# One transpose per up stage, additions split by bank, and three more couples by seven in a ConvGLU encoder on one Trainium2 core

## The chip, the core and the metric

The kernel runs on one core of one Trainium2 chip. A core has TensorE (PE: matmuls, with a separate row for its weight loads, PEld), VectorE (DVE), ScalarE (ACT), GpSimd (POOL), SyncE (SP, which issues transfers here) and sixteen DMA engines between the chip's memory and the core's own. The metric is the device time of one execution in microseconds (us), lower is better. The kernel before takes 2399.69 us, the median of three runs (2399.18 to 2400.01).

## What is computed

A trunk of two layers over 256 tokens and a model width of 2048, all in float32. Each layer adds a token mixer and then a gated MLP to the running sum `h`. The mixer is an mLSTM in layer 0 and an HGRN2 recurrence in layer 1. The change touches the MLP alone:

```python
def conv_glu(hn, w_up, conv_w, conv_b, w_down):
    u = hn @ w_up                                  # 2048 -> 2 * 5504
    a, v = jnp.split(u, 2, axis=-1)
    ap = jnp.pad(a, ((0, 0), (1, 1), (0, 0)))      # along the tokens
    c = conv_b
    for j in range(3):
        c = c + ap[:, j:j + s] * conv_w[j]
    return (jax.nn.gelu(c, approximate=False) * v) @ w_down

for layer in range(2):
    h = h + mixer(rmsnorm(h, norm_mix_g[layer]))
    h = h + conv_glu(rmsnorm(h, norm_ffn_g[layer]), ...)
return rmsnorm(h, final_g)
```

## The kernel before

**Float32 from two halves.** A weight tile `raw` is split into `wh` (rounded by ACT to TensorE's fast 32-bit format, line 170) and `wl` (the rest, by DVE, line 171), and the activations likewise into a high and a low half. A product is then three matmuls: high by high, high by low, low by high.

**Three parts.** The 5504 hidden columns are 43 tiles of 128, and an MLP works through them in three parts, of 16, 16 and 11 tiles. A part is an up stage and then a down stage.

**An up stage** has one chunk per tile. A chunk loads 2 MB of `w_up`, and for each of 16 blocks k of the model width issues, for its two outputs a and v, one matmul of 512 columns with `wh` (line 441: the high and the low half of the 256 tokens side by side) and one of 256 columns with `wl` (line 444). Such a couple of matmuls, 441 and 444, is called a *pair of matmuls* below: 32 in a chunk. When a chunk is done, DVE and ACT add the halves, apply the convolution, the GELU and the gate, and split the result for the down stage (`done_up`, lines 1107 to 1134).

**The transpose.** At a place that the table `RESETS` names (a chunk of the part and a k), line 428 issues one PE transpose of a constant identity into a scratch bank. Nobody reads it. It is one weight load and one matmul of 128 columns between two pairs of matmuls. The table before names two places per up stage.

**A down stage** multiplies the part's gated tiles by `w_down`, in two *pairs* of output columns (`Pair`, c = 0 for the first 1024 columns and c = 2 for the rest). `stream_pair` walks through the tiles two by two, by a plan with one letter for each couple of tiles:

- N: a couple in the plain way, eight products of 512 columns, 24 matmuls. H is a single tile, 12 matmuls.
- S: the same couple with seven products, 21 matmuls, from sums of the weights (`pair_sums`, lines 234 to 236, on DVE) and sums of the activations (`forms`, lines 459 to 466).
- P: as S, but the sums of the weights come ready from memory. They are made during the part's up stage, in halves: POOL fetches half of a couple's weights (`fetch_half`, lines 249 and 250) in one chunk, DVE and ACT make and split the sums in the next (`sum_half`, lines 257 to 260), and POOL stores them (line 262). The table `MAKE` names the chunks in which halves are fetched. In the down stage POOL loads the sums back, four transfers of 512 KB for each couple (line 282), into four buffers `pr0` to `pr3` that exist once.

A pair accumulates in four PSUM banks: `c11` and `c12` are the two banks of a tile `c1`, `c21` and `c22` of a tile `c2`. Two such tiles exist, so the next pair takes over the same ones. Three further banks m1, m6 and m7 hold products that the last S or P of the plan needs: after it, `middle` (lines 1156 to 1158 and 1182) combines them and adds them to `h` while the plan's remaining N and H run. At the pair's end `done` adds the four banks to `h` (line 1187, two additions of 1024 columns). In the second layer the last part has only the pair c = 0, and the remaining columns go by plain chunks.

**Order.** The order on each engine is fixed when the program is built: a scheduler places the instructions by its own estimate of their durations, and each engine then runs its list strictly in that order, waiting on semaphores. Weights are loaded by SP's queue into three buffers, in the order of the chunks; POOL's queue carries the fetches, stores and loads of the sums.

Of the kernel before, what the change touches and what calls it, by code (L numbers as in the profile page):

```python
# [12 lines left out]
ALU = mybir.AluOpType  # L13
# [5 lines left out]
KT = D // P  # L19
FT = 5504 // P  # L20
PARTS = ((0, 16), (16, 16), (32, 11))
RESETS = (((2, 1), (9, 1)), ((0, 3), (6, 1)), ((0, 3), (6, 1)))
A = "PSNSPSNN"
A2 = "PSNSPSNN"
B = "PSNNNH"
B2 = "PSNNNH"
DOWN_PLAN = {16: A, 11: B}
DOWN_PLAN2 = {16: A2, 11: B2}
MAKE = {16: (0, 2, 3, 5, 6, 8, 9, 11), 11: (0, 2, 3, 5)}
AH = 8  # L30
BH = 16
EPS = 1e-6
# [33 lines left out]
def trunk_kernel(ctx, tc, xT, x_d, fg_d, pp_d, cst_d, sel_d, w_gate, w_first, w_aq, w_ak, w_av, w_ao, w_aout,  # L66
                 w_bq, w_bv, w_bg, w_bout, w_up, w_down, w_last, out, mscr, sums):
    nc = tc.nc
    act, dve, pool, pe = nc.scalar, nc.vector, nc.gpsimd, nc.tensor
# [14 lines left out]
    hm = hx.rearrange("p k t -> p (k t)").rearrange("p (a c) -> p a c", a=2)  # L84
# [582 lines left out]
    def mlstm(norm, nxt, after):  # L667
# [23 lines left out]
        def gates(ps):  # L691
            with tc.tile_pool(name="gt", bufs=1) as gp:
# [18 lines left out]
                dve.tensor_tensor(lf, lf, e, ALU.add)  # L711
                B = gp.tile([H, T], F32, tag="l", name="B")
                pool.memset(B, 0.0)
                f_, b_ = slice(0, 32), slice(32, 64)
                scan = dve.tensor_tensor_scan
                scan(B[f_, 128:256], ones[f_, 128:256], lf[f_, 128:256], 0.0, ALU.mult, ALU.add)
                scan(B[f_, 126::-1], ones[f_, 0:127], lf[f_, 127:0:-1], 0.0, ALU.mult, ALU.subtract)
                scan(B[b_, 127::-1], ones[b_, 0:128], lf[b_, 127::-1], 0.0, ALU.mult, ALU.add)
                scan(B[b_, 129:256], ones[b_, 0:127], lf[b_, 128:255], 0.0, ALU.mult, ALU.subtract)
# [370 lines left out]
    def ffn(layer, norm, nxt):  # L1090
        stack = ExitStack()
        box = {}
        chunks = []
# [8 lines left out]
        def end():  # L1102
            box["prx"].__exit__(None, None, None)
            if last:
                nxt.begin(stack.enter_context(tc.tile_pool(name="fin", bufs=1)), sums_tile(box, "fg"))

        def done_up(f, i, GT, ahead):
            def go(ps):
# [23 lines left out]
                GT.half = None  # L1132
                if i in MAKE[GT.nf]:
                    j = MAKE[GT.nf].index(i)
                    if j // 2 < len(ahead):
# [25 lines left out]
        for part, (f0, nf) in enumerate(PARTS):  # L1161
            GT = Gated(nf)
            final = last and part == len(PARTS) - 1
            made = [{} for _ in range(2)]
            ahead = []
            for c in range(1 if final else 2):
                for i, kind in enumerate((DOWN_PLAN, DOWN_PLAN2)[c][nf]):
                    if kind == "P":
                        made[c][i] = numbers.pop()
                        ahead.append((made[c][i], w_down[layer, c][:, (f0 + 2 * i) * 1024:(f0 + 2 * i + 2) * 1024]))  # L1170

            for i in range(nf):
                chunks.append(Chunk("fm", w_up[layer, f0 + i], KT, norm.x, done_up(f0 + i, i, GT, ahead)))
                chunks[-1].reset = dict(RESETS[part]).get(i)
                chunks[-1].apart = bool(part) and i == 0
            for c in (0, 2):
                def middle(acc, c=c):
                    at = wpool.tile([P, 2048], F32, tag="raw", bufs=RAW, name="at").rearrange("p (t c) -> p t c", t=2)
                    combine(acc, at, 512)
                    for t in range(2):  # L1180
                        h = hm[:, t, 512 * c:512 * c + 1024]
                        dve.tensor_tensor(h, h, at[:, t], ALU.add)

                def done(acc, c=c, part=part):
                    for t in range(2):
                        h = hm[:, t, 512 * c:512 * c + 1024]
                        dve.tensor_tensor(h, h, acc["rows"][t], ALU.add)  # L1187
                    if part == len(PARTS) - 1:
                        if last or c:
                            end()  # L1190
                        nxt.add(c)
                        nxt.add(c + 1)
                if final and c == 2:
                    continue
                ch = Pair(w_down[layer, c // 2][:, f0 * 1024:(f0 + nf) * 1024], (DOWN_PLAN if c == 0 else DOWN_PLAN2)[nf], GT.get, GT.form, done, middle)
                ch.made, ch.box = made[c // 2], box
                chunks.append(ch)
            if final:
                def done(ps):
                    for t in range(2):  # L1200
                        h = hm[:, t, 1024:1536]
                        dve.tensor_tensor(h, h, ps[t], ALU.add)
                    nxt.add(2)
                for c in (2, 3):
                    chunks.append(Chunk("tm", w_last[c - 2], nf, GT.get, done))
                chunks[-1].last, chunks[-1].half = True, nxt.half
                chunks[-1].apart = chunks[-2].apart = True
# [15 lines left out]
    chunks = mlstm(n0, n1, begin0)  # L1223
    chunks += f0
    c = hgrn(n2, n3, begin1)
# [117 lines left out]
```

## Time and profile before

| What | Before |
|---|---|
| median of three runs | 2399.69 us |
| the profiled execution: its own time, its span | 2402.44 us, 2400.4 us |
| busy share of the span: PE, PEld, DVE, ACT, POOL | 99, 85, 81, 56, 13% |
| up stages of layer 0 (16, 16, 11 tiles), from | 402, 656, 916 us |
| down stages of layer 0, from and to | 574 to 656, 834 to 915, 1038 to 1097 us |
| up stages of layer 1, from | 1695, 1949, 2211 us |
| down stages of layer 1, from and to | 1867 to 1948, 2126 to 2210, 2333 to 2361 us |
| transposes of line 428 | 12, each with a duration of 0.27 us |
| clock granted to TensorE, mean | 0.998 of full speed |

The profile is of one execution. Matmuls overlap in it, so that the duration of one (0.39 us for 512 columns) is longer than the distance from its start to the next start, and a busy share of 99% says only that PE is never without an instruction. What a matmul costs is read from start to start.

### The profile page before, as it was taken

To read this page: it belongs to the slowest core of one execution; us is meant where nothing else is said; L and a number is where in the kernel's file an instruction comes from. 1 tells how busy PE (TensorE), PEld (TensorE's weight loads), DVE (VectorE), ACT (ScalarE), POOL (GpSimd) and SP (SyncE) were. 2 spreads that over 40 slices of the span, in tenths; PEclk is the share of its full clock that TensorE was granted. 3 is DMA by queue.
4 is the path that set the end of the run, shared out by engine and by line. 5 is a ranking of instruction groups with operands and counts; after the bars stand their busy time and mean duration, and the time that the engine had idled before them with its cause. 6 is when DMAs were issued, how large, how long until landed. Compare 5 with 4: busy or idle time off the path is not lost.

```text
span 2400.4 us, 37326 instructions
## 1 busy us (share of the span) xinstructions
PE 2383.1 (99%) x14212; PEld 2037.1 (85%) x14212; DVE 1940.4 (81%) x3197; ACT 1338.3 (56%) x2057; POOL 306.0 (13%) x451
## 2 busy tenths in 40 slices
PE   9999999999999999999999999999999999999998
PEld 7888888888888888888888888888888888887887
DVE  7766655888988888888888888885788888888876
ACT  6655455655556645655555555555565556654554
POOL 0100000111011110101222222220011101110100
PEclk9999999999999999999999999999999999999999
DMA  7655555888778887855455555445698768987854
GB/s 295 203 174 171 191 174 186 272 275 281 268 251 277 287 286 238 292 196 204 172 176 167 168 176 173 165 174 181 223 296 282 262 239 276 293 284 243 260 190 175
DMA packets 106019, 545.84 MB, mean 227 GB/s; under 512 B 10720, under 2 KB 11360, under 8 KB 55280
## 3 DMA queue, kind: packets, MB, share of 16 engines
q1 hardware_dynamic: 66656, 437.34, 53.2%
q0 software_dynamic: 38320, 104.94, 14.5%
q8 instruction: 111, 1.82, 0.3%
q10 hardware_dynamic: 864, 1.19, 0.1%
q14 instruction: 68, 0.56, 0.1%
HBM read 501.41 MB, written 42.01 MB: 226 GB/s over the span
## 4 chain that ended last, share of the span: by engine, by line
PE 96%; DVE 2%; DMA 2%; issue 0%; ACT 0%; SPq 0%; POOLq 0%; POOL 0%; ACTq 0%; DVEq 0%
PE mm L441 36%; PE mm L444 18%; PE c L309 11%; PE mm L422 7%; PE mm L423 7%; PE mm L424 7%; PE m L309 3%; DMA raw<-in_w_down 1%; DVE wl L171 1%; PE mm L433 1%; PE pn L790 1%; PE pd L973 1%; PE py L1022 1%; PE pz L536 0%; PE mm L435 0%
## 5 line engine op out<-in xcount | busy, mean ns | idle before, releaser
L441 PE MATMUL mm<-xt,wh 128*128 128x512 f32 x3690 | 1289.0, 395 | 0.0
L170 ACT CAST wh<-raw 128x1024 fp32r<-128x1024 f32 (+1 forms) x829 | 844.2, 1026 | 794.9 <-PE mm L441 471.7
L171 DVE TENSOR_TENSOR wl<-raw,wh 128x1024 fp32r<-128x1024 f32 (+1 forms) x829 | 989.8, 1199 | 357.8 <-ACT wh L170 351.0
L444 PE MATMUL mm<-xt,wl 128*128 128x256 f32 x3690 | 1027.1, 279 | 0.0
L441 PEld LDWEIGHTS mm<-xt,wh 128*128 128x128 f32 x3690 | 691.8, 188 | 158.4
L444 PEld LDWEIGHTS mm<-xt,wl 128*128 128x128 f32 x3690 | 693.7, 188 | 1.4
L309 PE MATMUL c<-wh,g 128*128 128x512 f32 x666 | 217.5, 390 | 0.0
L422 PE MATMUL mm<-wh,xt 128*128 128x512 f32 x480 | 188.2, 392 | 0.0
L423 PE MATMUL mm<-wl,xt 128*128 128x512 f32 x480 | 187.7, 391 | 0.0
L424 PE MATMUL mm<-wh,xt 128*128 128x512 f32 x480 | 187.3, 390 | 0.0
L309 PEld LDWEIGHTS c<-wh,g 128*128 128x128 f32 x666 | 125.2, 188 | 26.1
L309 PE MATMUL c<-wl,g 128*128 128x512 f32 x333 | 129.9, 390 | 0.0
L424 PEld LDWEIGHTS mm<-wh,xt 128*128 128x128 f32 x480 | 90.2, 188 | 18.5
L422 PEld LDWEIGHTS mm<-wh,xt 128*128 128x128 f32 x480 | 90.1, 188 | 18.5
L423 PEld LDWEIGHTS mm<-wl,xt 128*128 128x128 f32 x480 | 90.2, 188 | 17.4
L476 ACT COPY b<-mm 128x256 f32<-128x256 f32 x236 | 86.4, 366 | 20.5 <-DVE z L477 6.7
L170 ACT CAST wh<-T 128x1024 fp32r<-128x1024 f32 x54 | 55.3, 1050 | 69.7 <-PE c L309 43.3
L262 POOL DMA_DIRECT2D sums<-pr x76 | 53.0, 699 | 293.9 <-ACT pr L259 156.2
L282 POOL DMA_DIRECT2D pr<-sums x76 | 41.3, 551 | 359.5 <-PE c L309 244.5
L171 DVE TENSOR_TENSOR wl<-T,wh 128x1024 fp32r<-128x1024 f32 x54 | 64.8, 1223 | 26.0 <-ACT wh L170 25.7
L249 POOL COPY pr<-a 128x1 f32<-128x1 f32 x38 | 31.1, 819 | 424.2 <-DVE a L482 246.6
L309 PE MATMUL c<-wh,F 128*128 128x512 f32 x178 | 70.2, 394 | 3.8 <-DVE hx L1187 3.8
(274 smaller groups left out, 3022.7 us busy)
## 6 DMA issues: line engine op xcount, KB each, us to landing
raw<-in_w_up SPq DMA_DIRECT2D x172, 1024.0 KB, 5.6
raw<-in_w_down SPq DMA_DIRECT2D x60, 1024.0 KB, 6.1
raw<-in_w_bq SPq DMA_DIRECT2D x48, 1024.0 KB, 4.9
sums<-pr POOLq DMA_DIRECT2D x76, 512.0 KB, 8.1
pr<-sums POOLq DMA_DIRECT2D x76, 512.0 KB, 7.5
pr<-in_w_down POOLq DMA_DIRECT2D x38, 512.0 KB, 6.7
raw<-in_w_ao SPq DMA_DIRECT2D x16, 1024.0 KB, 4.9
raw<-in_w_aout SPq DMA_DIRECT2D x16, 1024.0 KB, 4.8
```

Of the source, the lines that this page charges most:

```text
L170: act.copy(h, r)
L171: dve.tensor_tensor(l, r, h.bitcast(F32), ALU.subtract)
L249: pool.tensor_copy(b[:, 0, 0:1], after)
L262: pool.dma_start(sums[n, j].rearrange("p (i o b) -> p i o b", i=2, o=2)[:, :, o], v.rearrange("p (i b) -> p i b", i=2))
L282: pool.dma_start(z[j], sums[n, j][:, 1024 * i:1024 * i + 1024])
L309: pe.matmul(o, a, b, start=name not in begun, stop=sp and i == 2)
L422: pe.matmul(ps[t], xh, wh[:, c], start=st, stop=False)
L423: pe.matmul(ps[t], xh, wl[:, c], start=False, stop=False)
L424: pe.matmul(ps[t], xl, wh[:, c], start=False, stop=sp)
L441: pe.matmul(ps[f], wh[:, c:c + P], x, start=st, stop=False)
L444: pe.matmul(ps[f][:, 0:T], wl[:, c:c + P], x[:, 0:T], start=False, stop=sp)
L476: act.copy(b, ps[:, T:2 * T])
```

## The change

```diff
-RESETS = (((2, 1), (9, 1)), ((0, 3), (6, 1)), ((0, 3), (6, 1)))
+RESETS = ((2, 1), (0, 3), (0, 3))
-B = "PSNNNH"
-B2 = "PSNNNH"
+B = "PSNPNH"
+B2 = "PSNPNH"
-MAKE = {16: (0, 2, 3, 5, 6, 8, 9, 11), 11: (0, 2, 3, 5)}
+MAKE = {16: (0, 2, 3, 5, 6, 8, 9, 11), 11: (0, 1, 2, 3, 4, 5, 6, 7)}
@@ the up stage's chunks
-                chunks[-1].reset = dict(RESETS[part]).get(i)
+                chunks[-1].reset = RESETS[part][1] if i == RESETS[part][0] else None
@@ the end of a pair
                 def done(acc, c=c, part=part):
-                    for t in range(2):
-                        h = hm[:, t, 512 * c:512 * c + 1024]
-                        dve.tensor_tensor(h, h, acc["rows"][t], ALU.add)
+                    for name, t, o, n in (("c12", 0, 512, 512), ("c11", 0, 0, 512), ("rows", 1, 0, 1024)):
+                        h = hm[:, t, 512 * c + o:512 * c + o + n]
+                        dve.tensor_tensor(h, h, acc["rows"][1] if n == 1024 else acc[name], ALU.add)
```

The change does three things. Each up stage has one transpose instead of two: the first of the two places stays and the second goes. The addition of `c1`'s two banks to `h` becomes two additions of 512 columns, `c12` first; that of `c2` stays one of 1024. In the parts of 11 tiles the fourth couple is done by seven products instead of eight, with sums from memory: two couples in layer 0 (one in each pair), one in layer 1. Their weights are summed in the up stage: the chunks 0 to 7 of layer 0's last part each fetch a half (before: 0, 2, 3 and 5), and chunks 0 to 3 in layer 1 (before: 0 and 2).

How this stands in the engines' lists is shown at four places. First PE at the start of layer 0's second up stage. `c` is the last bank of the down stage ahead, `mm` the up stage's PSUM tile, `turn` the transpose. Before:

```order
L309 MATMUL c_5788<-wh,g_5459 128x512
L441 MATMUL mm<-xt_3112,wh 128x512 x2
L428 MATMUL turn<-cst 128x128 x2
L444 MATMUL mm<-xt_3112,wl 128x256 x2
L441 MATMUL mm<-xt_3115,wh 128x512
```

And now:

```order
L309 MATMUL c_5787<-wh,g_5457 128x512
L441 MATMUL mm<-xt_3112,wh 128x512 x2
L428 MATMUL turn<-cst 128x128
L444 MATMUL mm<-xt_3112,wl 128x256 x2
L441 MATMUL mm<-xt_3115,wh 128x512
```

In the second and third up stage of either layer the two transposes stood next to each other, although the table names two chunks for them: nothing held the second back. One of the two is left, in the same place. In the first up stage of either layer, where they stood apart, the one in chunk 2 is left as it was and the one in chunk 9 is gone.

Second, PE at the start of the second pair in layer 0's first down stage, with the semaphores that an instruction waits for. `c_5787` (before) and `c_5786` (now) are the PSUM tile `c1`, taken over from the pair ahead; `m` are the further banks. Before:

```order
L309 MATMUL m_5789<-wh,g_3979 128x512 [waits Activation_49]
L309 MATMUL c_5787<-wh,F 128x512 [waits DVE_49]
L309 MATMUL c_5787<-wl,F 128x512
L309 MATMUL c_5787<-wh,g_3854 128x512
L309 MATMUL c_5788<-pr_5757,F 128x512 [waits DVE_49]
```

And now:

```order
L309 MATMUL m_5788<-wh,g_3979 128x512 [waits Activation_49]
L309 MATMUL c_5786<-wh,F 128x512 [waits DVE_49,PE_49]
L309 MATMUL c_5786<-wl,F 128x512
L309 MATMUL c_5786<-wh,g_3854 128x512
L309 MATMUL c_5787<-pr_5755,F 128x512 [waits DVE_49]
```

The products with F go into c12, the one with g_3854 into c11. There is a wait for DVE ahead of c12 and one ahead of c2, before and now, and none of its own ahead of c11.

Third, DVE at the end of the first pair of that stage: `T` is a tile of weight sums for the next pair, `hx` is `h`. Before:

```order
L1182 TENSOR_TENSOR hx<-hx,at 128x1024
L171 TENSOR_TENSOR wl<-raw,wh 128x512 [waits Activation_49]
L234 TENSOR_TENSOR T_5801<-raw 128x1024 [waits DMAHW0_49]
L1187 TENSOR_TENSOR hx<-hx,c_5462 128x1024 [waits DVE_49,PE_49]
L1187 TENSOR_TENSOR hx<-hx,c_5463 128x1024 [waits DVE_49,PE_49]
```

And now:

```order
L1182 TENSOR_TENSOR hx<-hx,at 128x1024
L171 TENSOR_TENSOR wl<-raw,wh 128x512 [waits Activation_49]
L234 TENSOR_TENSOR T_5800<-raw 128x1024 [waits DMAHW0_49]
L1187 TENSOR_TENSOR hx<-hx,c_5460 128x512 [waits DVE_49,PE_49]
L1187 TENSOR_TENSOR hx<-hx,c_5460 128x512
L1187 TENSOR_TENSOR hx<-hx,c_5461 128x1024 [waits DVE_49,PE_49]
```

The three additions stand behind the same instructions as the two did.

Fourth, POOL in the last up stage of layer 0: copies that order a fetch behind a chunk (line 249), fetches (250), stores (262). Before:

```order
L249 COPY pr0_8918<-a_8899 128x1
L250 DMA pr0_8918<-in_w_down 128x1024
L249 COPY pr0_9043<-a_9006 128x1
L250 DMA pr0_9043<-in_w_down 128x1024
L262 DMA sums<-pr2_9033 256x1x512
L262 DMA sums<-pr3_9034 256x1x512
L262 DMA sums<-pr2_9151 256x1x512
L262 DMA sums<-pr3_9152 256x1x512
```

And now:

```order
L249 COPY pr0_8814<-a_8777 128x1
L250 DMA pr0_8814<-in_w_down 128x1024
L262 DMA sums<-pr2_8804 256x1x512
L262 DMA sums<-pr3_8805 256x1x512
L249 COPY pr0_8932<-a_8902 128x1
L250 DMA pr0_8932<-in_w_down 128x1024
L262 DMA sums<-pr2_8922 256x1x512
L262 DMA sums<-pr3_8923 256x1x512
```

A fetch and two stores now follow each other in every chunk from 1 to 7, without a chunk in between that has none.

## The prediction

> **What bounds the kernel now.** I read the busy shares first, then the chain that ended last, then PE's waits.
>
> ```profile
> PE 2383.1 (99%) x14212; PEld 2037.1 (85%) x14212; DVE 1940.4 (81%) x3197; ACT 1338.3 (56%) x2057; POOL 306.0 (13%) x451
> PE 96%; DVE 2%; DMA 2%; issue 0%; ACT 0%; SPq 0%; POOLq 0%; POOL 0%; ACTq 0%; DVEq 0%
> ```
>
> PE has work for 99% of the span and is 96% of the chain. So a matmul less is time less, an edit on another engine counts only where PE then waits, and PE's waits are few:
>
> ```profile
> PE c L309 <- DVE hx L1187: 3.8, 4, 1.1
> PE m L309 <- ACT wh L170: 1.2, 1, 1.2
> ```
>
> Columns: us in total, times, longest. The first row is the wait at which the split additions aim: four times, 3.8 us in all. With PE so full, the distance between two matmul starts matters as much as their number, and that distance is not constant:
>
> ```profile
> 418.00:495.00 77.00, 77.00 (x223) 1.00 0.86 272
> 496.00:573.00 77.00, 77.00 (x219) 1.00 0.87 282
> 1711.00:1788.00 77.00, 77.00 (x223) 1.00 0.85 269
> 1789.00:1866.00 77.00, 77.00 (x219) 1.00 0.86 282
> 663.00:740.00 77.00, 77.00 (x223) 1.00 0.81 260
> 925.00:1002.00 77.00, 77.00 (x223) 1.00 0.80 258
> ```
>
> These windows count line 441 on PE: one per pair of matmuls. Same work, full clock (the 1.00), no idle, yet 223 or 219 pairs in 77 us, 345.3 (77.00/223) or 351.6 ns (77.00/219) each: a fast and a slow rhythm, 6.3 ns a pair apart. Slow are only the second halves of the two first up stages. The switch is at 495.63 and 1788.2, where the second transpose stands; the first transposes, at 417.87 and 1710.4, leave the rhythm fast.
>
> **The change part by part.** *Six transposes fewer.* Timeline of PE: start, duration, instruction.
>
> ```profile
> 417.51 0.40 PE L441 MATMUL mm<-xt,wh 128*128 128x512 f32 x1
> 417.87 0.27 PE L428 MATMUL turn<-cst 128*128 128x128 f32 x1
> 418.32 0.40 PE L441 MATMUL mm<-xt,wh 128*128 128x512 f32 x1
> 655.99 0.62 PE L441 MATMUL mm<-xt,wh 128*128 128x512 f32 x2
> 656.45 0.38 PE L428 MATMUL turn<-cst 128*128 128x128 f32 x2
> 656.90 0.39 PE L441 MATMUL mm<-xt,wh 128*128 128x512 f32 x1
> ```
>
> From 417.51 to 418.32 lie two pairs and one transpose: 0.81 us, less 0.69 for the pairs, 0.12. From 655.99 to 656.90 lie two pairs and two transposes: 0.91, so 0.11 each. Two times 0.12 and four times 0.11 is **0.7 us** off. (The Trainium skill, "TensorE: Matmul & The Clock Gate", section "Part 4: PE-mode transpose", gives some 275 ns for one inside a kernel. The duration here agrees, 0.27, but the starts are 0.11 to 0.12 apart; by the page's figure six would be an estimated 1.65 us.)
>
> *The rhythm after them.* In layer 0's first up stage the switch to slow came with the removed transpose. Without it 222 pairs stay fast: 222 x 6.3 ns = **1.4 us** off. In layer 1 it is less plain. The two switches have one thing in common beside the place: both transposes were even ones in the program's count (the 2nd and the 8th), and the first transposes, which switched nothing, odd (the 1st and 7th). A transpose is one weight load between matmuls that otherwise come in even numbers (354 in a down stage, 252 in a shorter one, 64 in a chunk), so each turns the parity of all that follows. Now there is one per stage, and the one in layer 1's first up stage is the 4th: even. If parity decides, it switches to slow, at chunk 2 rather than 9: 14 chunks less one pair, about 446 pairs slow where 222 were: 224 x 6.3 ns = **1.4 us** on. If place decides, these 222 become fast too. I take parity, as both switches bear it out; it is only two events.
>
> The second and third up stages begin fast with two transposes side by side (the windows from 663 and 925). One alone has not been seen there. I take it as fast, price 0, and give the other case below.
>
> *Nine matmuls fewer.* Three couples go from 24 to 21.
>
> ```profile
> 574.20:655.80 81.60, 80.63 (x354) 1.00 0.77 261
> 2336.00:2360.00 24.00, 24.00 (x108) 1.00 0.67 235
> ```
>
> Line 309's matmuls come 24.00/108 = 0.222 us apart where nothing waits, and 80.63/354 = 0.228 over a whole stage. Nine of 0.225 is **2.0 us** off.
>
> *The split additions.* The end of a pair, on DVE and PE:
>
> ```profile
> 605.72 0.68 DVE L1157 TENSOR_TENSOR at<-at,m 128x512 f32<-128x512 f32 x1
> 606.31 1.22 DVE L171 TENSOR_TENSOR wl<-raw,wh 128x1024 fp32r<-128x1024 f32 x1
> 616.45 2.35 DVE L1187 TENSOR_TENSOR hx<-hx,c 128x1024 f32<-128x1024 f32 x2
> 618.71 0.68 DVE L235 TENSOR_TENSOR T<-raw,T 128x512 f32<-128x512 f32 x1
> 617.72 0.50 PE L309 MATMUL c<-wh,F 128*128 128x512 f32 x1 [0.97 <-DVE hx L1187]
> 619.44 0.84 PE L309 MATMUL c<-pr,F 128*128 128x512 f32 x3
> ```
>
> Two additions of 1024 take from 616.45 to 618.71, 1.13 each; PE's first matmul into c12 starts at 617.72, as the first ends. An addition of 512 from PSUM takes 0.59 to the next start (605.72 to 606.31), two take 1.2. Were c12 free after its own 0.6, PE could start 0.55 earlier. But in the order of now, only c12's matmul waits for DVE; that into c11, three places later, has no wait of its own, though its bank must have been read. One wait then has to cover both banks, so it is for the second addition, and the split buys nothing: it costs 1.2 less 1.13, 0.07 us, at each of four waits, **0.3 us** on. Queued behind the waiting matmul is all of PE; c2's addition ends 0.07 later as well, at 618.8, and c2's matmul at 619.44 has that covered. (The Trainium skill, "Perfetto Trace Analysis", section "Optimizing Scalar/DVE Operations", puts the access overhead of a DVE instruction at some 125 ns on PSUM. That speaks against splitting: by it an estimated 0.5 us for the four. The trace's 0.07 is less.)
>
> *The added sums of weights.* The load falls on layer 0's last up stage, whose chunks take 11.1 us:
>
> ```profile
> 948.80:959.90 11.10, 11.10 (x66) 9.70 (x65) 9.01 (x17) 6.39 (x10) 0.74 (x2) 1.00 1.05 335
> 959.90:971.00 11.10, 11.10 (x66) 9.70 (x65) 10.11 (x18) 6.92 (x10) 3.01 (x4) 1.00 0.58 191
> 971.00:982.10 11.10, 11.10 (x66) 9.70 (x65) 10.19 (x21) 6.39 (x10) 0.06 (x1) 1.00 1.01 325
> 1004.30:1015.40 11.10, 11.10 (x66) 9.70 (x65) 8.36 (x15) 6.25 (x10) 1.14 (x3) 1.00 1.05 359
> L171 DVE TENSOR_TENSOR wl<-raw,wh 128x1024 fp32r<-128x1024 f32 x39 | 47.7, 1224 | 18.7 <-ACT wh L170 18.1
> L260 DVE TENSOR_TENSOR pr<-pr,pr 128x1024 fp32r<-128x1024 f32 x4 | 4.9, 1218 | 0.0
> L234 DVE TENSOR_TENSOR pr<-pr 128x512 f32<-128x512 f32 x4 | 2.8, 690 | 0.3
> L235 DVE TENSOR_TENSOR pr<-pr,pr 128x256 f32<-128x256 f32 x4 | 1.7, 417 | 0.0
> L236 DVE TENSOR_TENSOR pr<-pr,pr 128x256 f32<-128x256 f32 x4 | 1.7, 419 | 0.0
> ```
>
> The window rows give PE, PEld, DVE, ACT and POOL busy, the clock, and DMA's share and GB/s. The second and third chunk hold a half's sums on DVE, the other two none: 10.1 to 10.2 us busy of 11.1 against 8.4 to 9.0. From the groups, a half is (4.9 + 2.8 + 1.7 + 1.7)/4 = 2.8 us, four more are 11 of the 18.7 us that DVE idles ahead of line 171 in this stretch. It fits, with 0.9 us free in each of eight chunks. The memory: a chunk's 2.1 MB of weights, a fetch of 0.52 and two stores of 0.52 make 3.7 MB in 11.1 us, 331 GB/s for seven chunks running; 325 to 359 were moved in single chunks, with a share of 1.01 to 1.05. So it fits barely, covered by three buffers loaded ahead. The sums' loads are the third risk: they are issued when a buffer comes free, and
>
> ```profile
> pr<-sums POOLq DMA_DIRECT2D x4, 512.0 KB, 9.2
> ```
>
> (issues in 594 to 600, median to landing) 9.2 us is 41 matmuls of 0.225, about the distance from release to need where the second P now follows an N and an S. Lower bound 0 (all covered), upper bound one landing uncovered by half in one pair plus a late chunk, some 3 us. I take **0.5 us** on, near the lower end, since DVE has its 0.9 us free in each chunk.
>
> *Sum.* -0.7 - 1.4 + 1.4 - 2.0 + 0.3 + 0.5 = -1.9 us. The profiled execution's own time is 2402.44, 2.75 over the median, and one stretch holds nearly all of that:
>
> ```profile
> 2126.40:2210.50 84.10, 82.19 (x353) 0.98 0.74 254
> 2172.00:2175.00 3.00, 3.00 (x9) 2.35 (x8) 3.00 (x5) 1.04 (x1) 0.02 (x1) 0.50 0.53 224
> ```
>
> This down stage took 84.1 us against 81.6 for its twin above, with PE idle for 1.9 and then a granted clock of 0.50 for three us, after a late load. The timed runs lack it. 2402.44 - 1.9 = 2400.5 for an execution with that event; without its 2.75, **2397.8 us**.
>
> **Rivals.** *Place, not parity:* layer 1's first up stage is fast throughout. For it: both switches stood in chunk 9, at k = 1, and no transpose in chunk 2 switched. Against it: the matmuls around are alike in all four places. Instead of 1.4 on it is 1.4 off: 2395.0 us.
>
> *A lone transpose leaves the second and third up stages slow* (the other side). There are 512 and 352 pairs in them, all fast now behind a doubled transpose, which leaves the parity as it was. At 6.3 ns these are 3.2 and 2.2 us. One layer so is 5.4 on, 2403.2 us; both 2408.6 us. It decides against the change from about 300 slow pairs more (1.9 us/6.3 ns), less than one such stage. For it: a transpose did switch to slow twice. Against it: it did not twice, and in these stages it stands at the very start, behind another rhythm.
>
> *Layer 0's last part runs short:* DVE at over 92% or 331 GB/s for seven chunks do not hold, and PE waits where weights come late. At the upper bound of 3 us instead of 0.5: 2400.3 us, no gain.
>
> *The split does work:* c12's matmul starts 0.55 earlier, though c2's additions, now 0.07 later, soon hold PE again; worth 0.2 to 0.4 at each wait, instead of 0.07 on: 2397.8 - 0.3 - 1.2 = 2396.3 us. Against it stands the missing wait ahead of c11.
>
> **How the numbers follow.** The forecast has 0.42, place 0.22, the lone transpose 0.20 (one layer 0.15, both 0.05), the short part 0.10, the working split 0.06. About 0.2%, 4.8 us, is what a measurement of this kernel can tell from no change: 2394.9 to 2404.5. The likeliest case alone has 2396.5 to 2400.3, by the bounds of its 0.5 us and half a us elsewhere. The range reaches down past "place", with its neighbours, to 2393.5, and up past the lone transpose in one layer to 2404.5; outside lie both layers and the tails. Faster: half of "place" and some tails where two gains meet, 0.20. Slower: both layers, a third of one layer, 0.11. The rest, 0.69, is no change that can be told.
>
> **What would show it.** Line 441 counted in 77 us windows: 223 after 496 right for layer 0's first stage; 219 soon after 1711 for parity, 223 for place; 219 after 663 or 925 for the lone transpose. PE's wait for line 1187: four times about 1.0 to 1.1, or less if the split works. In layer 0's last up stage no wait of PE, or one for line 171's `wl` or a load. Layer 0's last down stage shorter by 1.4 us (six matmuls), layer 1's by 0.7 (three). Wrong would be the forecast if the down stages' matmuls took a rhythm of their own, or if the rhythm of the HGRN2 stage moved with the parity, which I left at nothing.

## The result and the profile after

The changed kernel takes **2418.89 us**, the median of six runs (2414.24 to 2422.77); the kernel before, run beside it, 2400.12 us. The ratio is 1.0076, with a 95% interval of 1.0061 to 1.0090: the change costs about 18 us. Forecast were 2397.8 us and a range up to 2404.5. The page of the profiled execution, 2418.7 us:

```profile
span 2416.9 us, 37462 instructions
PE 2392.0 (99%) x14197; PEld 2037.8 (84%) x14197; DVE 1957.8 (81%) x3252; ACT 1344.2 (56%) x2067; POOL 325.5 (13%) x487
PE 92%; DVE 4%; DMA 3%; issue 1%; ACT 1%; SPq 0%; POOLq 0%; POOL 0%; ACTq 0%; DVEq 0%
```

The lines are the span, the busy time of each engine, and the chain that ended last. PE has fifteen matmuls fewer (14212 before) and is busy 9 us longer, and 4 points of the chain (96 to 92) have gone to others, 3 of them to DVE and DMA. Both point to the distance between matmuls and to PE's waits.

The span from stage to stage, worked out from the start of each stage's first matmul in the two traces (us):

| Stage | Before | After | Difference |
|---|---|---|---|
| start to the first down stage | 574.19 | 572.71 | -1.48 |
| layer 0, first down stage | 81.80 | 82.29 | +0.49 |
| layer 0, second up stage | 177.72 | 181.00 | +3.28 |
| layer 0, second down stage | 81.84 | 82.08 | +0.24 |
| layer 0, third up stage | 122.26 | 124.26 | +2.00 |
| layer 0, third down stage | 59.10 | 67.27 | +8.17 |
| mixer of layer 1 and its first up stage | 769.85 | 769.21 | -0.64 |
| layer 1, first down stage | 81.90 | 81.76 | -0.14 |
| layer 1, second up stage | 177.72 | 181.00 | +3.28 |
| layer 1, second down stage | 84.36 | 82.08 | -2.28 |
| layer 1, third up stage | 122.26 | 124.36 | +2.10 |
| layer 1, third down stage | 28.57 | 28.58 | +0.01 |
| the rest | 38.82 | 40.27 | +1.45 |

They sum to the 16.5 us between the two spans. The -2.28 is the late load that only the profiled execution of before had. Two groups carry the rest: the second and third up stages of both layers, **10.7 us**, and the last down stage of layer 0, **8.2 us** with six matmuls fewer. The row of layer 1's mixer holds two things: its first up stage is 1.60 us shorter (179.93 before, 178.33 after), and the mixer is 0.96 longer. The mixer differs by about that much between kernels that leave it as it is (589.6 to 590.5 us), so the 0.96 is not put down to the change. At the end came 1.5 us for which the forecast had no term.

The rhythm first. Windows of line 441 on PE, after:

```profile
496.00:573.00 77.00, 76.76 (x222) 1.00 0.88 288
1789.00:1866.00 77.00, 77.00 (x224) 1.00 0.90 289
663.00:740.00 77.00, 77.00 (x219) 1.00 0.81 256
925.00:1002.00 77.00, 77.00 (x219) 1.00 0.87 280
1970.00:2047.00 77.00, 77.00 (x219) 1.00 0.80 257
2234.00:2311.00 77.00, 77.00 (x219) 1.00 0.89 290
```

The first up stages (the upper two) are fast to their ends in both layers, where 219 stood before. The second and third, 223 before, are slow. A window also counts the matmul that runs into it from before, so 77 us over the count is a little too short a distance: from start to start a pair takes 346.7 ns in the fast rhythm and 353.3 in the slow, 6.6 apart and not 6.3.

Then PE's longest waits in the whole program, of after. Below them stands the last down stage of layer 0 by line 309 (the window, PE's busy time and count, the clock, DMA's share, GB/s), first of before, then of after:

```profile
PE c L309 <- DVE hx L1187: 6.0, 5, 1.6
PE m L309 <- DMA pr<-sums: 3.4, 3, 2.2
PE m L309 <- DVE wl L171: 1.5, 1, 1.5
```

```profile
1037.82:1096.91 59.09, 58.43 (x252) 1.00 0.59 213
```

```profile
1042.34:1109.61 67.27, 61.01 (x246) 0.97 0.82 286
```

The loads of the sums (`pr<-sums`) are a wait that did not exist. The timeline of PE shows a wait for DVE's `wl` four us into the stage and the loads' from six us on, and the window of PE behind them a granted clock of 0.58:

```profile
1046.89 0.50 PE L309 MATMUL m<-wl,g 128*128 128x512 f32 x1 [1.51 <-DVE wl L171]
1050.48 1.22 PE L309 MATMUL m<-pr,F 128*128 128x512 f32 x2 [2.15 <-DMA pr<-sums]
1054.49 0.50 PE L309 MATMUL m<-pr,F 128*128 128x512 f32 x1 [0.66 <-DMA pr<-sums]
```

```profile
1050.00:1053.00 3.00, 2.52 (x6) 0.58 1.04 386
```

With six matmuls fewer (1.35 us at 0.225) the stage lost 9.5 us. The start distances that hold its waits make up 7.0 of them beyond the usual 0.227 each, six matmuls at half clock 1.2, and many small differences the rest.

POOL's timeline says why the loads are late. These are the first and the fourth of the four loads for the plan's first couple, of before and of after:

```profile
1000.97 0.54 POOL L282 DMA_DIRECT2D pr<-sums  x1 [12.06 <-DVE pr L236]
1015.65 0.53 POOL L282 DMA_DIRECT2D pr<-sums  x1 [3.43 <-DMA sums<-pr]
```

```profile
1036.57 0.55 POOL L282 DMA_DIRECT2D pr<-sums  x1 [6.99 <-DVE pr L236]
1048.66 0.53 POOL L282 DMA_DIRECT2D pr<-sums  x1 [0.85 <-DMA sums<-pr]
```

Before, they were issued 37 to 22 us ahead of the stage (1037.8); now 6 us ahead to 6 us behind its start (1042.3). What they wait for stands in the brackets: the last half's sums on DVE (line 236), which free pr0, and the last half's store, which frees pr3. The first couple's sums had been in memory for long; it is the buffers that were not free.

### The profile page after: what moved, and what is told of

The parts are those of the page before. It is cut to its first block, busy times and chain, and to the rows that moved or that the text cites. A ratio compares the mean times of both kernels' runs of the same rounds, so it can differ in the third digit from the quotient of the medians.

```text
span 2416.9 us, 37462 instructions
## 1 busy us (share of the span) xinstructions
PE 2392.0 (99%) x14197; PEld 2037.8 (84%) x14197; DVE 1957.8 (81%) x3252; ACT 1344.2 (56%) x2067; POOL 325.5 (13%) x487
## 3 DMA queue, kind: packets, MB, share of 16 engines
q0 software_dynamic: 44176, 120.67, 16.5%
## 4 chain that ended last, share of the span: by engine, by line
PE 92%; DVE 4%; DMA 3%; issue 1%; ACT 1%; SPq 0%; POOLq 0%; POOL 0%; ACTq 0%; DVEq 0%
PE mm L441 35%; PE mm L444 18%; PE c L309 9%; PE mm L422 7%; PE mm L423 7%; PE mm L424 7%; PE m L309 3%; DVE wl L171 2%; DMA raw<-in_w_down 1%; PE mm L433 1%; PE pn L790 1%; PE pd L973 1%; PE py L1022 1%; ACT wh L170 1%; DVE hx L1182 0%
## 5 line engine op out<-in xcount | busy, mean ns | idle before, releaser
L309 PE MATMUL c<-wh,g 128*128 128x512 f32 x612 | 203.0, 390 | 0.0
L309 PEld LDWEIGHTS c<-wh,g 128*128 128x128 f32 x612 | 115.0, 188 | 24.6 <-ACT v L1155 0.5
L309 PE MATMUL c<-wl,g 128*128 128x512 f32 x306 | 119.5, 391 | 0.0
L282 POOL DMA_DIRECT2D pr<-sums x88 | 48.0, 553 | 413.1 <-PE c L309 286.8
L262 POOL DMA_DIRECT2D sums<-pr x88 | 61.1, 696 | 252.8 <-ACT pr L259 141.9
L309 PE MATMUL c<-wh,F 128*128 128x512 f32 x196 | 76.7, 392 | 6.0 <-DVE hx L1187 6.0
```

The lines of the kernel that those rows point to most:

```text
L262: pool.dma_start(sums[n, j].rearrange("p (i o b) -> p i o b", i=2, o=2)[:, :, o], v.rearrange("p (i b) -> p i b", i=2))
L282: pool.dma_start(z[j], sums[n, j][:, 1024 * i:1024 * i + 1024])
L309: pe.matmul(o, a, b, start=name not in begun, stop=sp and i == 2)
```

## The experiments

The theory drawn from these two profiles had two parts: a lone transpose leaves the second and third up stages slow (10.7 us), and the first couple's sums in layer 0's last down stage come late because the last of eight halves is late (8 to 9 us). Times below are medians, each against that of the kernel before from the same chip.

### Each part taken back

`e1` puts the second transposes back:

```diff
-RESETS = ((2, 1), (0, 3), (0, 3))
+RESETS = (((2, 1), (9, 1)), ((0, 3), (6, 1)), ((0, 3), (6, 1)))
```

> The changed kernel with the two transposes per up stage put back; the couples and the split additions stay changed. Theory (two separate losses: the slow rhythm of the second and third up stages behind a lone transpose, 3.3 + 2.0 + 3.3 + 2.1 us, and late sums for the first couple of layer 0's last down stage, 8 to 9 us): the rhythm of all up stages is that of the kernel before, the last down stage of layer 0 still takes about 67 us instead of 59, and the time is about 8 us over before, near 2408 us. Rival (the couples alone disturb everything behind them, the transposes hardly matter): the time stays near 2418 us.

Measured: 2412.15 us against 2400.79, ratio 1.0041 (1.0028 to 1.0054). The second and third up stages are back at 177.72 and 122.26 us to the hundredth; layer 0's last down stage takes 67.80. The rival, 2418, is out. Over the theory's 2408 it lies by two things left out of that figure: 1.4 us more at the program's end, as in the changed kernel, and in the profiled execution a further stretch at half clock behind a pair's end in layer 1 (that down stage took 84.0 us). Layer 0's last down stage is not made up as in `after`: PE waits 3.8 us for the loads and 0.7 for `wl`, and 10.2 us of the stage, not 3.4, ran at half clock.

`e2` puts the old couples back:

```diff
-B = "PSNPNH"
-B2 = "PSNPNH"
-MAKE = {16: (0, 2, 3, 5, 6, 8, 9, 11), 11: (0, 1, 2, 3, 4, 5, 6, 7)}
+B = "PSNNNH"
+B2 = "PSNNNH"
+MAKE = {16: (0, 2, 3, 5, 6, 8, 9, 11), 11: (0, 2, 3, 5)}
```

> The changed kernel with the old couples (plans and chunks of the sums as before); one transpose per stage and the split stay. Theory: the last down stage of layer 0 is back at 59 us, the second and third up stages of both layers stay slow (181 and 124 us instead of 177.7 and 122.3): 10.6 us on, some 3.0 off for the first up stages and 0.7 for the transposes, about 7 us over before, near 2407 us. Rival (the rhythm hangs on the changed down stages, not on the transposes): fast up stages, near 2397 us.

Measured: 2409.80 us, ratio 1.0033 (1.0022 to 1.0044). Up stages 181.00 and 124.36 us, the last down stage of layer 0 60.94. That stage takes 59.10 to 60.94 us in the seven profiles with the old couples and their old chunks, so a us of difference in it says nothing. Windows of line 441:

```profile
663.00:740.00 77.00, 77.00 (x219) 1.00 0.79 255
925.00:1002.00 77.00, 77.00 (x219) 1.00 0.79 255
```

So the two losses are separate, and each goes with its own part: transposes with the rhythm, couples with the last down stage.

`e3` is the kernel before with the split additions alone.

```diff
-                    for t in range(2):
-                        h = hm[:, t, 512 * c:512 * c + 1024]
-                        dve.tensor_tensor(h, h, acc["rows"][t], ALU.add)
+                    for name, t, o, n in (("c12", 0, 512, 512), ("c11", 0, 0, 512), ("rows", 1, 0, 1024)):
+                        h = hm[:, t, 512 * c + o:512 * c + o + n]
+                        dve.tensor_tensor(h, h, acc["rows"][1] if n == 1024 else acc[name], ALU.add)
```

> The kernel before with the split additions alone. Theory (the matmul into c12 waits for the second addition): PE's waits at the four pair ends grow by about 0.07 us each, to 1.1 us, up to 0.5 us each if the two additions also start later; 2400.4 us, at most 2402. Rival (the split frees c12 early): the four waits shrink to 0.5 us, 2398.5 us.

Measured: 2400.95 against 2400.79, ratio 0.9999 (0.9990 to 1.0008): no change that can be told. The trace can tell it. DVE's additions and PE's first matmul into c12:

```profile
616.69 2.41 DVE L1187 TENSOR_TENSOR hx<-hx,c 128x512 f32<-128x512 f32 x3
618.12 0.47 PE L309 MATMUL c<-wh,F 128*128 128x512 f32 x1 [1.16 <-DVE hx L1187]
```

From the first addition's start to the matmul are 1.43 us; before it was 617.72 - 616.45 = 1.27. With the split it is 1.42 to 1.43 in `after`, `e1` and `e2` too, at the same place; without it, 1.27 in `e4`. The matmul waits for the second addition, as the order said, and the price is 0.15 us a wait.

### The transposes alone

`e4` is the kernel before without the second transpose of the first up stages:

```diff
-RESETS = (((2, 1), (9, 1)), ((0, 3), (6, 1)), ((0, 3), (6, 1)))
+RESETS = (((2, 1),), ((0, 3), (6, 1)), ((0, 3), (6, 1)))
```

> The kernel before with one transpose in the first up stage of either layer and two in the second and third. Theory (what counts is only what stands in the stage itself): the first up stages are fast throughout, the second and third stay fast behind two transposes: 2 x 1.5 us off, near 2397 us. Rival (an odd number of transposes since the mixer shifts the rhythm that the later stages start from, and two side by side leave it as it is): the second and third up stages become slow, by up to 10 us: near 2407 us.

Measured: 2397.81 us, ratio 0.9985 (0.9976 to 0.9994). The first up stages are fast to their ends, the others stay at 177.82 and 122.26 us. This is the gain that the change contained.

`f4` has none at all, `g2` three in the second and third up stages (the third lands at the head of the second chunk):

```diff
-RESETS = (((2, 1), (9, 1)), ((0, 3), (6, 1)), ((0, 3), (6, 1)))
+RESETS = ((), (), ())
```

```diff
-RESETS = (((2, 1),), ((0, 3), (6, 1)), ((0, 3), (6, 1)))
+RESETS = (((2, 1),), ((0, 3), (6, 1), (7, 1)), ((0, 3), (6, 1), (7, 1)))
```

> The kernel before without any transpose. Theory (a lone transpose shifts the rhythm, two side by side leave it as none would): all up stages fast, 2 x 1.4 us for the first ones and 1.3 us for twelve transposes off, 2396 us. Rival (the stages start in a rhythm that two transposes mend): the second and third up stages slow, 5.4 us a layer, 2407 us.

> The kernel of e4 with three transposes in the second and third up stages: two side by side at the start, one at the head of the second chunk. Theory (a lone transpose shifts the rhythm one step, fast to slow, wherever it stands behind a fast one): both stages slow from the second chunk on, 2407 to 2408 us. Rival (two or more at the start put the rhythm right for the stage): both fast, 2398 us.

Measured: `f4` 2408.59 us, ratio 1.0028 (1.0017 to 1.0040); `g2` 2405.03 in its one run. Line 441 in `f4`, second and third up stage of layer 0, then in `g2` the same of both layers:

```profile
663.00:740.00 77.00, 77.00 (x219) 1.00 0.81 259
925.00:1002.00 77.00, 77.00 (x219) 1.00 0.80 255
```

```profile
663.00:740.00 77.00, 77.00 (x219) 1.00 0.81 259
925.00:1002.00 77.00, 77.00 (x224) 1.00 0.81 260
1970.00:2047.00 77.00, 77.00 (x219) 1.00 0.81 259
2234.00:2311.00 77.00, 77.00 (x223) 1.00 0.78 252
```

Without any transpose these stages are slow as well, in both layers, while the first up stages are fast to their ends: the theory that two side by side are as good as none has fallen, and its rival stands, that they start in a rhythm which two mend. With three, the second stage is slow and the third fast, in both layers, so neither "each shifts by one" nor "two or more are enough" holds. What is shown is a table: 0, 1, 2, 3 transposes give slow, slow, fast, slow in the second up stage, and slow, slow, fast, fast in the third. With three the place differs too, since the third stands a chunk later. By what state of PE it goes is left open.

### The couples

Three kernels on the base of `e4` ask what makes the sums late.

`f1` takes the fourth couple in the first pair alone, with six halves:

```diff
-B = "PSNNNH"
+B = "PSNPNH"
-MAKE = {16: (0, 2, 3, 5, 6, 8, 9, 11), 11: (0, 2, 3, 5)}
+MAKE = {16: (0, 2, 3, 5, 6, 8, 9, 11), 11: (0, 1, 2, 3, 4, 5)}
```

> The kernel of e4 (one transpose in the first up stage, two in the others) with the fourth couple by seven in the first pair alone: one couple in layer 0, one in layer 1; six halves in a row, in chunks 0 to 5. Theory (the sums of the first couple come late because the four buffers are busy until the last half is stored): with the last half two chunks earlier no wait for loads in layer 0's last down stage, 58.4 to 60 us; each layer 0.7 off; POOL's drain at the program's end 7.7 us instead of 5.0, if it goes by the loads of the last stage (8 instead of 4), 1.4 to 1.9 on at the end; 2398.3 us. Rival (halves in every chunk overload DVE and the memory): that stage over 64 us, 2403 us.

`f2` is `f1` with the last stage's second four loads on SP's queue:

```diff
-                        pool.dma_start(z[j], sums[n, j][:, 1024 * i:1024 * i + 1024])
+                        q = nc.sync if ch.by_sp and c else pool
+                        q.dma_start(z[j].bitcast(F32), sums[n, j][:, 1024 * i:1024 * i + 1024].bitcast(F32))
```

> As f1, with the second couple's four loads of the program's last down stage issued by SP instead of POOL. Theory (the drain at the end goes by POOL's transfers of the last stage): drain back at 5.0 us, 2396.5 us. Rival (it goes by all of POOL's transfers in the program, 15 more than in e4 less these 4): drain near 6.0 us, 2398 us.

`f3` leaves the couples as they were and only makes their sums later:

```diff
-MAKE = {16: (0, 2, 3, 5, 6, 8, 9, 11), 11: (0, 2, 3, 5)}
+MAKE = {16: (0, 2, 3, 5, 6, 8, 9, 11), 11: (4, 5, 6, 7)}
```

> The kernel of e4 with the old couples and the old number of halves, but fetched in chunks 4, 5, 6 and 7 of the parts of 11 tiles instead of 0, 2, 3 and 5. Theory (late sums): layer 0's last down stage takes 65 to 68 us instead of 59 to 61, with PE waiting for the sums' loads, 2404 to 2406 us. Rival (eight halves instead of four are what DVE and the memory can't carry): that stage stays at 59 to 61 us, 2398 us.

Measured: `f1` 2397.99 (ratio 0.9986, 0.9976 to 0.9995), `f2` 2398.16 (0.9983, 0.9974 to 0.9993), `f3` 2402.66 (1.0000, 0.9990 to 1.0010). Layer 0's last down stage, `f1` and then `f3`, and the first and fourth load of the first couple in `f3`:

```profile
1036.43:1096.97 60.54, 58.66 (x249) 1.00 0.71 245
```

```profile
1036.76:1102.02 65.26, 61.00 (x252) 0.97 0.67 230
```

```profile
1024.20 0.55 POOL L282 DMA_DIRECT2D pr<-sums  x1 [6.93 <-DVE pr L236]
1038.55 0.53 POOL L282 DMA_DIRECT2D pr<-sums  x1 [1.64 <-DMA sums<-pr]
```

Six halves in a row, made early, cost that stage no wait for a load longer than 0.2 us; its 60.54 us lie above the 58.4 to 60 expected, and with three matmuls fewer than `e4` (60.66) it is no shorter. Four made late, no more work than before, cost it 4.6 us over `e4`. Of these, 1.6 are PE's waits for the loads; a wait of 1.6 for `wl` in the second pair (0.6 in `e4`) and 3.4 us at half clock behind it make up most of the rest, and whether late sums cause these is not shown. This execution is also the longest of `f3`'s eight, 3.7 us over their median. The medians on the same chip, 4.7 us apart, agree with the stage. So the time of the last half counts, with no half more than before; whether eight halves are too much besides, `f3` can't say. In `f2` the drain at the end was not 5.0 but 6.4 us; more on that below.

Two tries to get eight halves through went wrong, each in its own way. `g1` lets the halves use another buffer, so that two of the four that the loads go to are free early:

```diff
-        b = spare(0, box).bitcast(F32).rearrange("p (a b) -> p a b", a=4)
+        b = spare(4, box).bitcast(F32).rearrange("p (a b) -> p a b", a=4)
-        t, th, tl = (spare(i, box) for i in (1, 2, 3))
-        t = t.bitcast(F32)
+        th, tl = (spare(i, box) for i in (2, 3))
+        t = tl.bitcast(F32)
```

> The kernel of e4 with the fourth couple by seven in both pairs of the parts of 11 tiles (eight halves in chunks 0 to 7, as in the changed kernel), but the halves use one further buffer and two of the four that the loads go to, so that the first couple's first two loads need not wait for the last half; the other two still do. Theory (late sums): layer 0's last down stage takes 61 to 64 us instead of 67, 2400 us with the longer drain at the end. Rival (eight halves overload DVE and the memory, whatever the buffers): 67 us, 2404 us.

Measured: 2471.20 us, ratio 1.0283 (1.0264 to 1.0301). Waits of DVE and of PE:

```profile
DVE pr L257 <- DMA sums<-pr: 101.4, 26, 8.7
PE mm L444 <- DVE wl L171: 21.2, 10, 4.4
```

The sum and its low half now share one buffer, so the next half's sum cannot begin until the store has landed, and DVE, which works strictly in order, stands there with the weights behind it. This is a flaw of the experiment and says nothing on the question; it shows what one wait at the head of DVE's list costs.

`g3` exchanges the first two couples, so that the sums are needed 21 matmuls later:

```diff
-B = "PSNNNH"
-B2 = "PSNNNH"
-MAKE = {16: (0, 2, 3, 5, 6, 8, 9, 11), 11: (0, 2, 3, 5)}
+B = "SPNPNH"
+B2 = "SPNPNH"
+MAKE = {16: (0, 2, 3, 5, 6, 8, 9, 11), 11: (0, 1, 2, 3, 4, 5, 6, 7)}
```

> The kernel of e4 with the couples of the changed kernel, eight halves, and the first two couples of each plan of the parts of 11 tiles exchanged (S P N P N H): the couple whose sums are loaded is needed 21 matmuls, 4.8 us, later. Theory (late sums): layer 0's last down stage 62 to 64 us instead of 67, about 2401 us. Rival (eight halves overload DVE, and an S at the start, whose sums DVE makes there, adds to it): 67 us or more, over 2404 us.

Measured: 2413.28 us, ratio 1.0046 (1.0031 to 1.0061); the stage 70.65 us, and the up stage ahead 126.68 instead of 122.26. My theory's 62 to 64 missed, and the rival's figures came; but the plan's new S at the start is part of that rival, so the run doesn't say which of the two it was. DVE in that up stage, of `g3`, and then of `after`:

```profile
1017.80 0.69 DVE L234 TENSOR_TENSOR pr<-pr 128x512 f32<-128x512 f32 x1 [5.10 <-DMA pr<-in_w_down]
```

```profile
1021.11 0.69 DVE L234 TENSOR_TENSOR pr<-pr 128x512 f32<-128x512 f32 x1 [4.51 <-DMA pr<-in_w_down]
```

DVE waits 4 to 5 us at the head of a half's sums for a fetch that has not landed. It does so in `after`, `e1`, `g3` and a little in `f3`, and not in `before` or `f1`. A link was missing in the theory: the next fetch goes into the same pr0 and is issued only when DVE has read the last one. In `after` the eight fetches are issued from 932.1 to 1025.8, 13.4 us apart on the mean (10.7 to 17.0), where a chunk takes 11.3. On the mean each half falls 2 us further behind, until DVE, whose list has the sums at a fixed place, stands in front of one.

`h1` gives pr0 a second copy, with eight halves and the plan of the change:

```diff
-        return box["pr"].tile([P, 1024], F32R, tag=f"pr{i}", bufs=1, name=f"pr{i}")
+        return box["pr"].tile([P, 1024], F32R, tag=f"pr{i}", bufs=1 if i else 2, name=f"pr{i}")
```

> The kernel of e4 with the couples of the changed kernel (eight halves) and a second copy of the buffer pr0, into which halves are fetched. Theory (the halves form a chain, fetch, landing, sums, next fetch, through the one buffer, about 13.4 us a half against a chunk of 11.1, so that eight fall 15 us behind, the loads of the sums come late, and DVE stands behind fetches that have not landed): fetches about 11 us apart, no wait of DVE for a fetch, the last half 10 us earlier or more; layer 0's last down stage 59 to 62 us instead of 67 to 68; 2398 to 2400 us. Rival (DVE's load of eight halves is the cause): 66 us or more, over 2404 us.

Measured: 2404.97 us (2398.97 to 2408.06), ratio 1.0013 (1.0004 to 1.0023), over the theory's 2400 and at the rival's 2404. The profiled execution is the fastest of the ten, 6 us under their median, and where the others spent these 6 us is not shown. Its first and last fetch, and what PE still waits for:

```profile
926.20 0.53 POOL L250 DMA_DIRECT2D pr<-in_w_down  x1 [0.30 <-DVE v L477]
1007.75 0.55 POOL L250 DMA_DIRECT2D pr<-in_w_down  x1 [0.30 <-POOL pr L249]
```

```profile
PE m L309 <- DMA pr<-sums: 4.5, 3, 2.4
```

Fetches are 11.65 us apart (seven steps in 81.55), DVE's wait for one is down to 1.4 us, and PE has no wait for DVE in that stage beyond the pair's end. The stage takes 64.66 us: 3 better than `e1`'s 67.80, still 4 over `e4`. But PE waits 4.5 us for the loads, not less than in `e1` (3.8); what is gone against `e1` is the wait for `wl` and the stretch at half clock. The loads are issued up to 1037.5, three us into the stage, and while the last fetch is issued 27 us ahead of the stage, against 17 in `after`, the last half's sums end only 9 us ahead of it, against 6 (7 in `e1`). That half was fetched at 1007.75, and DVE begins on it at 1021.12 without a wait for it: here the place in DVE's list sets the time, not the buffer. So the chain through pr0 explains DVE's stand in front of a fetch and two or three us of the lateness. Most of the rest goes with the last half's place in chunk 7, as in `f3`; that the load of eight halves has a part in it is not ruled out.

`i1` is `f1`, six halves, with the second copy of pr0; `i2` is `e4`, four halves and the old couples, with it. The edit is that of `h1`.

> The kernel of f1 (one transpose in the first up stages, two in the others; the fourth couple by seven in the first pair alone, six halves) with the second copy of pr0 from h1. Theory (what remained in h1, waits of 4.5 us for the sums' loads, comes from the last of eight halves being stored only at the stage's start; with six there is time): no wait for loads, layer 0's last down stage 58 to 60 us; the four pairs' ends keep the shorter waits of h1 (0.6 to 0.8 us less each); 2394.5 to 2396.5 us. Rival (a couple more in layer 0 costs in any case what it saves): 2397.5 us or more.

> The kernel of e4 (old couples, four halves) with the second copy of pr0. Theory (the shorter waits at the pairs' ends in h1 come from the second buffer, which lets loads and DVE's work fall earlier): the four down stages of 16 tiles 80.3 to 81.3 us, 2395 to 2396 us. Rival (they come from the order that the new couples bring): 81.6 us each, 2397.8 us.

Measured: `i1` **2395.07 us** (2392.41 to 2398.27) against 2400.51, ratio 0.9978 (0.9970 to 0.9987); `i2` 2395.63, ratio 0.9982 (0.9972 to 0.9991). In `i1`, the first and the last load of that stage's first couple:

```profile
989.90 0.54 POOL L282 DMA_DIRECT2D pr<-sums  x1 [4.83 <-DVE pr L236]
1019.23 0.53 POOL L282 DMA_DIRECT2D pr<-sums  x1 [2.03 <-DMA sums<-pr]
```

They are 44 to 15 us ahead of the stage (1034.0), which takes 59.66 us; PE waits for no load in it. `i1` is faster than both kernels, by 5.4 us than the one before. That a sixth half or the second buffer is worth anything over `e4` is not shown: the intervals of `e4`, `i1` and `i2` overlap. With six halves the second buffer doesn't bring the last one forward either: POOL's load behind its sums is issued 92.1 us after the up stage's start in `i1` and 91.7 in `f1`. What it does at the pairs' ends stays unclear: the four down stages of 16 tiles take 80.3 to 81.9 us in `i1` and 80.8 to 81.9 in `i2`, not the 80.3 to 81.3 that I had expected.

## Why the prediction was wrong

**What bounds the kernel** was read rightly: PE, and the rhythm as much as the count. Two of the rivals came true at once, which no case of the forecast had added up: the lone transpose in both layers (priced at 10.8 us, measured 10.7) and the short part (priced at 3 us in all, measured 9.5 with its six matmuls).

**Transposes.** 0.12 us for a lone one stands: the two pairs around the one at 417.98 take as long as before. Right in size, and nothing beside what follows.

**The rhythm of the first up stages.** Layer 0's 1.4 us came: the stage is 1.60 us shorter, 222 pairs of 6.6 ns and one transpose. Layer 1's came too, where 1.4 us on had been forecast. Parity of the program's count fell at once: the 4th transpose, an even one, switched nothing, and layer 1's first up stage is fast (224 in the window after 1789). The rival "place" had that right. Two events had been too few to prefer a rule.

**The second and third up stages.** This is the step that failed: "One alone has not been seen there. I take it as fast, price 0". It rested on reading a pair of transposes as neutral, from the parity that had been guessed for other stages. `f4` shows that they are not neutral but needed: with none the stages are slow as with one. In `after` they lost 3.28 and 2.00 us in layer 0, 3.28 and 2.10 in layer 1, where the forecast had nothing. What sets the rhythm stays open. The profile of before could not show it, since it had no stage of that kind with another number; the honest price was the rival's 5.4 us a layer with a chance near one half.

**Nine matmuls.** Their 2.0 us are not visible as such. Layer 1's last down stage is as long as before although 3 of 126 went, since two matmuls of the plain chunks (line 422) now stand inside it and some others came 231 to 338 ns apart instead of 227. From that stage's first matmul to PE's last are 57.82 us against 58.27: 0.45 of the 0.7.

**The split additions.** The mechanism was right, read from the order: one wait covers both banks. Its size was 0.15 us instead of 0.07. The sum of the durations gives the forecast's 0.07: the second short addition ends 1.28 us after the first one's start (0.60 to its own start, 0.68 long), the long one ended after 1.21. The other 0.08 lies between an addition's end and the matmul, 0.06 us before and 0.14 now, which the sum had taken as equal; why it grew is not shown.

**The added sums.** The other step that failed: "I take 0.5 us on, near the lower end, since DVE has its 0.9 us free in each chunk". The working asked whether DVE and the memory could carry eight halves on the mean, and the up stage itself bears it: it takes 122.26 us in `e1` and `h1`, as before. What was not worked out was when the last half ends, since only then the buffers of the loads are free. The term was 0.5 us, its upper bound 3; the stage lost 9.5. The risk in the loads was sought at the second couple of sums; it was the first, whose loads stand behind the last half for want of buffers. From `before`'s four halves in chunks 0, 2, 3 and 5 this could have been seen: there, too, the first load waited for line 236 of the last half, at 1000.97, 37 us ahead of need. In `after` it is issued 6 us ahead. Of the 31 us lost some 23 are the two chunks by which the last half is fetched later (chunk 7 instead of 5, 11.3 us each); the rest is drift, to which the one buffer belongs (13.4 us a half against a chunk of 11.3). `f3`, late without more halves, has the waits for loads; `f1`, with six early ones, has not. How much the load of eight halves adds by itself stays open.

**The end of the program** had no term at all: 1.9 us for POOL's drain, told below.

## What to carry to other kernels

When a kernel makes something ahead of time through shared buffers, price the latest item, not only the load: find when the last item is made and when it lets go of what the first consumer needs, by the place of its work in each engine's order and by its way from buffer to buffer, and compare with the slack that the first consumer had. An instruction without effect on data that a tuned kernel carries may set a rhythm; a count of them is tried stage by stage, and a rule from two events is no ground for a price of nothing. And where one wait covers two banks, splitting the work ahead of it only made it longer here.

## What the runs showed of the hardware

POOL's last DRAIN grew with the number of transfers that POOL issued in the whole program, in all runs but one. Instructions of the program's last line, of before and of after (durations in ns: least, median, longest):

```profile
L1325 POOLq DRAIN  x3: 46/102/5014, 2393.8 to 2400.1; - x3
```

```profile
L1325 POOLq DRAIN  x3: 46/102/7709, 2408.4 to 2416.6; - x3
```

There were 76 + 76 + 38 = 190 transfers of sums and their weights before and 220 after (and 20 others in either): 2.70 us for 30, 0.09 each. In `f1` there were 210 and the drain took 6.73 us (0.086 each), in `f2` 206 and 6.40 (0.087 each); so in these runs it goes by all transfers, and not by those of the last stage, as I had expected of `f2`. The count is not the whole rule: in `g1`, with 220, the drain took 1.50 us. What differs there is left open. Before, the drain ended 0.8 us ahead of what then ended the program, and cost nothing; now it ends the program, and from PE's last matmul to the end are 11.0 us instead of 9.1, 1.9 more.

Up-stage matmuls of one shape, at full clock and without a wait, come 346.7 or 353.3 ns a pair apart for a whole stage or the rest of one, by the transposes that stand in it, and the number needed for the fast rhythm differs from stage to stage.

PE's clock fell after short gaps: in `after` to 0.50 of full for the 3.4 us from 1050.5 on (the 0.58 above is a mean that takes in full speed), behind gaps of 1.5 and 2.2 us, with matmuls 427 ns apart instead of 227. In `e1` it was 0.50 for 10.2 us at the same place. In `h1` gaps of 1.0 and 2.4 us there were followed by no fall. The Trainium skill, "TensorE: Matmul & The Clock Gate", section "Part 1: The HAM clock gate (the "warmup" mystery)", has the clock halved after an idle window of some 3.4 us whose phase is free-running. The half rate agrees (0.50, 427 ns); the length does not, since in `after` no gap ahead of the fall was longer than 2.2 us. That `h1` shows no fall would fit a free-running phase, but no run here shows the phase.
